# A wider pitch for the split value weights, and one set of five places for the sums of two passes

## The chip, the cores and the metric

The kernel runs on one core of one Trainium2 chip. The metric is the device time of one execution, in microseconds.

## The reference, cut to what matters

One hybrid encoder layer runs over two token sets with shared weights: a long one (1024 tokens, "A" in the kernel) and a short one (512 tokens, "B"). All is float32.

```python
def encoder_layer(x, pre_w, w_in, ...):
    h = rms_norm(x, pre_w)
    cols = jnp.einsum('bsd,dc->bsc', h, w_in)
    m_qk, m_v, m_o, m_z, m_i, m_f, a_qkv, a_z, gate = jnp.split(cols, ..., axis=-1)
    y_m = mlstm_mixer(m_qk, m_v, m_o, m_i, m_f, ...) * silu(m_z)
    y_a = dilated_attention(a_qkv, rel_table) * silu(a_z)
    merged = sig(g[:, :, 0]) * (y_m @ w_pm) + sig(g[:, :, 1]) * (y_a @ w_pa)
    return x + rms_norm(merged @ w_out, post_w)
```

The change concerns one part of `h @ w_in` for the long set: the 2576 columns that are wanted with tokens on the partitions. These are 16 gate columns (i, f), the 1024 value columns of the mLSTM and the 1536 value columns of the attention. The kernel calls them the values.

## The kernel before, in words

**Precision.** A float32 product is made of three matmuls (`mm3`, L212 to L214): each operand is split into a high part, rounded by a copy on ScalarE, and a low part, the rest, by a subtraction on DVE. High times high, high times low and low times high are summed in PSUM.

**Values of the long set, about the first 236 us.** The 1024 x 1024 input of the long set and the weights are taken as 2 x 2 blocks, and a block product by seven products in place of eight (a Strassen-like form; the seven combinations of input blocks are `B11, T2, B21, T3, T1, T4, B22`, high and low parts in `H[0]` and `H[1]`, 512 columns a row). The value columns are computed in four groups of 644 (`value_group`, g = 0 to 3), each of two halves of `VW = 322`. A group needs seven combinations of weights, each `[128, 4 x 322]`: four k slices of 322 columns. Each combination is split into a pair of tiles "vhi" and "vlo" (`split`, ScalarE at L466, DVE at L467); there are two buffers of each, so that one is split while the other is multiplied. In `product` the parts of H are the stationary operand, 128 columns of it, and a k slice of "vhi" or "vlo" is the moving one: 4 token tiles x 4 slices x 3 matmuls = 48 matmuls of 322 columns a product. A token tile's sum fills one of eight PSUM banks ("d").

**The sums.** The products of a group are combined in tiles "u2" (four a group) and "u3" (four a group). ScalarE copies the first product into "u2" (L588 in group 0, L619 later), DVE adds others (L610, L633, L651, L670). At the end of a group `out` writes them: gate columns by a copy (L505), mLSTM values split once more into "vz" or "vzm" (L511, L512) and stored from there, attention values stored straight from the sum by SP (L516). Groups 0 and 2 use four tiles "u2", groups 1 and 3 four tiles "u2b". Group 0 also keeps four sums "held" (L599) for later, in tiles "u2b", and before that "u2b" serves for four small diagonal matrices (`diag`, L383) at the very start.

**Memory of this stage.** Pool "vw" lies on the left, behind the pool of the H tiles. It holds, in this order, "vhi" x2, "vlo" x2, "va", "vb", "vsum" (raw weights and their combinations, 10304 bytes a partition each). The pools "x0" (four rows of tokens, later replaced by "more") follow on the left. On the right lies "us" (small norms, "u2", "u2b"), and beside it "x1", later "co".

**The next stage: pairs.** Behind the values, all other projections of the long set are computed by pairs of units. Its pool "pairs" opens on the left once "vw" has been given back, so on the same bytes. A tile there waits for the users of the earlier tiles on its own bytes and for no others. `pair_weights` allocates, in this order, two "pu2" and one "pu3" of 2048 bytes, two "phlb" of 8192, four "pw_raw" of 4096, two "phla" of 8192 and two "psum_w" of 4096, loads the weights of two units into two "pw_raw" (L691, issued by SP, with high priority), splits the first unit's into "phla" (`pair_split`, ScalarE at L677, DVE at L678), and forms sums of both on POOL (L696, L697, L699) into "psum_w", which are split into the second "phla". `unit_pair` then multiplies: the first product takes the first "phla", the second one the split "psum_w". The weights of the first pair are called for ahead of the last sums of group 3 (L670), which are issued on DVE behind the split of "psum_w":

```python
coming = N.pair_weights(U_AQ, U_AQ + 1, sb)
with tc.issue_after(N.split_end.ins):
    for _ in values[3]:
        pass
for x in late:
    with tc.issue_after(coming[1].ins):
        nc.sync.dma_start(*x)
```

The stores that belong to the last two products of group 3 (list `late`, eight of them, issued at L2084) come behind the load of the pair's second unit.

**Order.** The order of TensorE's instructions is that of the program throughout this part. The order on DVE, ScalarE, POOL and SP is made when the kernel is built, by a list scheduler that plays the program through with estimated times; every engine then works its list in order.

Of the kernel before, what the change touches and what calls it, by code (L numbers as in the profile page):

```python
# [22 lines left out]
F32 = mybir.dt.float32  # L23
F32R = mybir.dt.float32r
AF = mybir.ActivationFunctionType
# [4 lines left out]
P = 128  # L30
D = 1024
KT = D // P
BLK = 512
# [12 lines left out]
VS, NV = 430, 2580  # L46
RING = 1024
VW = 322
U_MQ, U_MK, U_MV, U_MO, U_MZ = 0, 8, 16, 24, 32
U_AQ, U_AK, U_AV = 40, 52, 64  # L50
U_AZ, U_GA, U_GB = 76, 80, 88
# [132 lines left out]
class Net:  # L184
# [264 lines left out]
    def value_weights(self, sb):  # L449
        return [sb.tile([P, 2, 4 * VW], F32, name=x, bufs=1) for x in ("va", "vb", "vsum")]  # L450

    def value_group(self, g, T, H, sb, us, co, ps, late=None, begin=None, u3=None, more=None, turn=None):

# [1 line left out]
        nc = self.nc  # L457
        store = nc.sync.dma_start
        N = 4 * VW
        place = lambda: [sb.tile([P, N], F32R, name=x, bufs=2) for x in ("vhi", "vlo")]  # L460
        def split(x, at=None, parts=1):
            hi, lo = at or place()
            with self.tc.high_priority():
                for i in range(parts):
                    c = slice(i * N // parts, (i + 1) * N // parts)
                    ends = (nc.scalar.activation(hi[:, c], x[:, c], AF.Copy),  # L466
                            (nc.gpsimd if i else nc.vector).tensor_sub(lo[:, c], x[:, c], hi[:, c].bitcast(F32)))  # L467
            self.splits = ends
            return hi.rearrange("p (k c) -> p k c", c=VW), lo.rearrange("p (k c) -> p k c", c=VW)

        def opening(g):
            wa, wb = (sb.tile([P, 2, N], F32, name=x, bufs=1) for x in ("va", "vb"))
# [26 lines left out]
        def out(t, blk, jc, c):  # L499
# [15 lines left out]
            if a0 < hi:  # L515
# [1 line left out]

        vz = lambda: (more.tile([P, 2, VW], F32R, name="vzm", bufs=2) if more and next(turn) < 2 else
                      co.tile([P, 2, VW], F32R, name="vz", bufs=3))
        tile_ = lambda name, bufs: (us if name[:2] == "u2" else co).tile([P, VW], F32, name=name, bufs=bufs)  # L520
        u2 = [tile_(("u2", "u2b")[g % 2], 4) for _ in range(4)]
        add = nc.vector.tensor_add
        if g == 0:
            lead()
# [68 lines left out]
            with self.tc.issue_after(low[0]):  # L593
                sub(T1)
            m2 = product(B21, w12, with_m2(), onto=m1)
            held = []
            for t in range(4):
                held.append(tile_("u2b", 4))
                nc.scalar.activation(held[t], m2[t][:, :VW], AF.Copy)  # L599
            m7 = product(T3, w7, with_m7())  # L600
            with self.tc.issue_after(low[1]):
# [11 lines left out]
            co = co()  # L613
        else:
# [10 lines left out]
            co = co()  # L625
            for t in range(4):
                c = tile_("co", 3)
# [1171 lines left out]
    def place(self, which, i, dt=F32R):  # L1799

        return self.take((("V0b", "V1b", "K0", "K1"), ("H0", "H1", "H2", "H3"))[which][i], dt).rearrange("p (k t) -> p k t", k=4)
# [183 lines left out]
def body(tc, a):  # L1985
# [3 lines left out]
    with ExitStack() as st:  # L1989
# [12 lines left out]
        with ExitStack() as s1:  # L2002
# [4 lines left out]
            with ExitStack() as sv:  # L2007
                vw = N.pool(sv, "vw", 1, "left")
                us = N.pool(s2, "us", 1, "right")
                s3, s4 = ExitStack(), ExitStack()  # L2010
                begin = [vw.tile([P, 4 * VW], F32R, name=x, bufs=2) for x in ("vhi", "vlo")], *N.value_weights(vw)
                r = [us.tile([P, 6], F32, name=f"xr{t}") for t in range(6)]
                one = us.tile([P, VW], F32, name="u2", bufs=4)[0:1, :P]
                diag = [us.tile([P, VW], F32, name="u2b", bufs=4)[:, :P] for _ in range(4)]
                xp = N.pool(s3, "x0", 1, "left"), N.pool(s4, "x1", 1, "right")
                xt = [[xp[i].tile([P, D], F32, name=f"x{i}{t}") for t in range(4)] for i in range(2)]
                minus, plus = (H[1][T4][:, 3, i * P:(i + 1) * P] for i in range(2))
                spare = H[0][T4].bitcast(F32).rearrange("p a c -> p (a c)")
                row, pw = spare[0:1, D:], spare[:, :D]
                rows = lambda i, t: nc.sync.dma_start(xt[i][t], A.x[i * BLK + t * P:i * BLK + (t + 1) * P])  # L2020
                weights = lambda j, kh: nc.sync.dma_start(begin[1 + j][:, kh], a["w_vp"][0, j, kh])
                nc.scalar.dma_start(row, a["prew"][0:1])
                nc.scalar.dma_start(N.prew, a["prewc"])
                for t in range(4):
                    rows(0, t)
                weights(0, 0)
                for t in range(4):
                    rows(1, t)
                for j, kh in ((0, 1), (1, 0), (1, 1)):
                    weights(j, kh)  # L2030
                nc.vector.memset(one, 1.0)
                for i in range(2):
                    p = ps.tile([P, BLK], F32, name="d")
                    nc.tensor.matmul(p, one, row[:, i * BLK:(i + 1) * BLK], start=True, stop=True)
                    nc.vector.tensor_copy(pw[:, i * BLK:(i + 1) * BLK], p)
                nc.scalar.activation(minus, N.ident, AF.Copy, scale=-1.0)
                nc.scalar.activation(plus, N.ident, AF.Copy)
                opened = []

                def co():  # L2040
                    if not opened:
                        s4.close()
                        opened.append(N.pool(s2, "co", 1, "right"))
                    return opened[0]

                def again():
                    H[0][T4] = place("h", T4)

                turns = N.combos(ps, H, xt, r, H[1][T4][:, :2].rearrange("p a c -> p (a c)"), pw, plus, minus, again, diag)
                values = [N.value_group(0, A, H, vw, us, co, ps, None, (*begin, turns), [x[:, :VW] for x in xt[0]])]  # L2050
                next(values[0])
                N.small(N.const)
                N.gate_sums(A, hp)
                N.gate_tile(A, N.const)
                for _ in values[0]:
                    pass
                s3.close()
                more, turn = N.pool(sv, "more", 1, "left"), itertools.cycle(range(5))
                values += [N.value_group(g, A, H, vw, us, co, ps, late if g == 3 else None, more=more, turn=turn)
                           for g in range(1, 4)]  # L2060
                next(values[1])
                with ExitStack() as s4:
                    lanes = N.lanes(A, N.pool(s4, "lane", 1, "right"), lambda: ps.tile([P, BLK], F32, name="d"))
                    for g in range(1, 3):
                        for j, _ in enumerate(values[g]):
                            if j % 3 == 0:
                                with tc.issue_after(N.splits[0].ins), tc.issue_after(N.splits[1].ins):
                                    next(lanes, None)
                    for _ in lanes:
                        pass  # L2070
                    with tc.issue_after(N.splits[0].ins):
                        N.halved()
                    N.bias_tables(N.pool(s4, "tab", 1, "right"), ps, dram)
                for _ in range(7):
                    next(values[3])
# [205 lines left out]
```

## Time and profile before

| | us |
|---|---|
| median of 3 runs | 2209.26 |
| lowest, highest | 2207.99, 2214.44 |
| profiled execution | 2210.35 |
| its span, first to last instruction | 2208.6 |

The page and the answers drawn from the trace are read as follows. A line of a timeline gives the start in us, the duration in us, the engine, the line of the kernel, the operation, the tile written and the tiles read ("out<-in", buffer numbers left out), the shapes, the count, and in brackets the idle time of the engine before it and what ended that. PE is TensorE's matmul, PEld its weight load, ACT ScalarE, DVE VectorE, POOL GpSimd, SP SyncE, "SPq" an engine's DMA-issuing queue. A line of a table by tile or source gives duration min/median/max in ns and the first and last start. Matmuls overlap: a duration is longer than the distance between two starts, and it is the distance that counts. Tiles "u2" of the code stand as "u" in many lines of the trace, since lists of tiles share a name.

### The profile page before, as it was taken

How to read it: one execution, taken by the hardware profiler on the slowest of the kernel's cores; microseconds unless marked ns; L12 is line 12 of the kernel's file. 1: busy time of each engine (PE TensorE's matmuls, PEld its weight loads, DVE VectorE, ACT ScalarE, POOL GpSimd, SP SyncE). 2: the span in 40 equal slices, each digit the busy share in tenths (PEclk: the TensorE clock that was granted, in tenths of full speed). 3: DMA queues.
4: the chain of work that ended last, by engine and by line, in shares of the span. 5: the costliest groups of instructions: out<-in, count | busy, mean ns of one | idle time of the engine just before them, and what ended most of it. 6: DMA issues, size and time to landing. Idle time of an engine off the chain costs nothing.

```text
span 2208.6 us, 34775 instructions
## 1 busy us (share of the span) xinstructions
PE 2188.1 (99%) x12106; PEld 1895.0 (86%) x12106; DVE 1488.0 (67%) x2973; ACT 1102.8 (50%) x2294; POOL 714.5 (32%) x1005
## 2 busy tenths in 40 slices
PE   9999999999999999999999999999999999999998
PEld 8999888888888888888888889998788888888787
DVE  7775675657777656547888765564689845665674
ACT  7332334444444333446676666666666644544332
POOL 1000432333333222326777640011155522232221
PEclk9999999999999999999999999999999999999999
DMA  3742443423323222375745569996868696686663
GB/s 125 194 115 80 158 162 131 172 105 115 115 105 115 86 80 85 132 255 200 242 154 202 160 193 253 249 233 182 256 224 273 198 276 213 214 266 195 233 218 109
DMA packets 209146, 390.45 MB, mean 177 GB/s; under 512 B 37417, under 2 KB 123113, under 8 KB 208970
## 3 DMA queue, kind: packets, MB, share of 16 engines
q1 hardware_dynamic: 179128, 279.63, 40.1%
q0 software_dynamic: 26240, 96.00, 13.8%
q10 hardware_dynamic: 3602, 12.59, 1.4%
q8 instruction: 96, 1.57, 0.3%
q14 instruction: 80, 0.66, 0.1%
HBM read 274.70 MB, written 113.44 MB: 176 GB/s over the span
## 4 chain that ended last, share of the span: by engine, by line
PE 93%; DMA 2%; DVE 2%; ACT 1%; issue 1%; POOL 0%; SPq 0%; DVEq 0%; POOLq 0%; ACTq 0%
PE d L214 14%; PE d L212 14%; PE d L213 14%; PE dense L212 12%; PE dense L213 12%; PE dense L214 12%; PE lg L1486 2%; PE num L214 1%; PE num L212 1%; PE num L213 1%; PE pt L1516 1%; PE a L1095 1%; PE kv L212 1%; PE kv L213 1%; PE kv L214 1%
## 5 line engine op out<-in xcount | busy, mean ns | idle before, releaser
L212 PE MATMUL dense<-H,wh 128*128 128x512 f32 x664 | 270.0, 407 | 0.0
L214 PE MATMUL dense<-H,wl 128*128 128x512 f32 x664 | 260.6, 392 | 0.0
L213 PE MATMUL dense<-H,wh 128*128 128x512 f32 x664 | 260.6, 392 | 0.0
L213 PE MATMUL d<-Hl,phla 128*128 128x512 f32 x608 | 236.5, 389 | 0.0
L214 PE MATMUL d<-Hh,phla 128*128 128x512 f32 x608 | 236.5, 389 | 0.0
L212 PE MATMUL d<-Hh,phla 128*128 128x512 f32 x608 | 236.5, 389 | 0.0
L281 DVE TENSOR_TENSOR wl<-wraw,wh 128x1024 fp32r<-128x1024 f32 (+1 forms) x121 | 148.8, 1231 | 61.2 <-ACT wh L275 61.0
L212 PE MATMUL d<-Hh,phlb 128*128 128x512 f32 x456 | 177.4, 389 | 0.0
L213 PE MATMUL d<-Hl,phlb 128*128 128x512 f32 x456 | 177.4, 389 | 0.0
L214 PE MATMUL d<-Hh,phlb 128*128 128x512 f32 x456 | 177.4, 389 | 0.0
L275 ACT ACTIVATE wh<-wraw 128x1024 fp32r<-128x1024 f32 (+1 forms) x124 | 128.2, 1035 | 69.0 <-PE dense L213 26.3
L214 PEld LDWEIGHTS dense<-H,wl 128*128 128x128 f32 x664 | 124.7, 188 | 27.9
L696 POOL TENSOR_TENSOR psum_w<-pw_raw 128x512 f32<-128x512 f32 x38 | 54.6, 1436 | 282.9 <-DMA pw_raw<-w_in 252.2
L214 PE MATMUL d<-vhi,Hl 128*128 128x322 f32 x448 | 140.5, 314 | 0.5 <-DVE Hl L432 0.3
L212 PE MATMUL d<-vhi,Hh 128*128 128x322 f32 x448 | 140.3, 313 | 0.1
L213 PE MATMUL d<-vlo,Hh 128*128 128x322 f32 x448 | 139.6, 312 | 0.0
L212 PEld LDWEIGHTS dense<-H,wh 128*128 128x128 f32 x664 | 125.1, 188 | 16.0 <-issue 1.2
L213 PEld LDWEIGHTS dense<-H,wh 128*128 128x128 f32 x664 | 125.3, 189 | 14.4
L214 PEld LDWEIGHTS d<-Hh,phla 128*128 128x128 f32 x608 | 114.1, 188 | 23.7
L212 PEld LDWEIGHTS d<-Hh,phla 128*128 128x128 f32 x608 | 114.1, 188 | 23.7
L213 PEld LDWEIGHTS d<-Hl,phla 128*128 128x128 f32 x608 | 114.1, 188 | 23.6
L1505 DVE CUSTOM_DVE_ANT_0 ls<-lg,bias 128x256 f32<-128x256 f32 (+2 forms) x240 | 78.7, 350 | 79.7 <-PE lg L1486 57.9
(605 smaller groups left out, 5945.5 us busy)
## 6 DMA issues: line engine op xcount, KB each, us to landing
pw_raw<-w_in SPq DMA_DIRECT2D x76, 512.0 KB, 4.1
wraw<-w_in SPq DMA_DIRECT2D x63, 512.0 KB, 4.5
aqk_a<-pwk SPq DMA_DIRECT2D x40, 512.0 KB, 3.5
wraw<-w_pm POOLq DMA_DIRECT2D x24, 512.0 KB, 5.7
wraw<-w_out POOLq DMA_DIRECT2D x24, 512.0 KB, 4.0
aqk_b<-sw SPq DMA_DIRECT2D x40, 256.0 KB, 5.9
wraw<-w_v POOLq DMA_DIRECT2D x22, 430.0 KB, 6.3
qk_a<-pwk SPq DMA_DIRECT2D x16, 512.0 KB, 2.6
```

What stands on the lines that cost most here:

```text
L212: nc.tensor.matmul(out, lh, rh, start=start, stop=False, **kw)
L213: nc.tensor.matmul(out, lh, rl, start=False, stop=False, **kw)
L214: nc.tensor.matmul(out, ll, rh, start=False, stop=stop, **kw)
L275: high = nc.scalar.activation(hi[:, :n], raw[:, :n], AF.Copy)
L281: low = (self.lows or nc.vector).tensor_sub(lo[:, :n], raw[:, :n], hi[:, :n].bitcast(F32))
L696: self.nc.gpsimd.tensor_add(s[:, 0], ws[1][:, 0], ws[1][:, 1])
L1095: nc.tensor.matmul(p[:, c - c0], kT[:, ct, c * P:(c + 1) * P], qT[:, ct, c * P:(c + 1) * P], start=ct == 0, stop=ct == 1)
L1486: nc.tensor.matmul(lg[:, hh], q[hh][:, qs], z.rearrange("p (n j) -> p n j", j=P)[:, pair], start=z is k[hh], stop=z is not k[hh])
L1505: nc.vector.tensor_tensor_reduce(out=ls[rows, hh], in0=ts["lg"][hh][rows, of], in1=bt[rows, hh, by], scale=1.0, scalar=NEG, op0=OP.add, op ...
L1516: nc.tensor.transpose(pp[:, hh * nk + x], ts["ls"][:, hh, x * P:(x + 1) * P], self.ident)
```

## The change

The tiles "vhi" and "vlo" get 4 x 384 columns, of which each k slice uses 322; `split` writes 4 runs of 322 and slices k where it sliced columns. The tag "u2b" is gone: all groups take their four sums from one tag "u2" with five places in rotation. The four `diag` matrices come from the same tag. `held` is written into the second halves of the token rows `xt[0]`, beside "u3" of group 0, which is in their first halves as before.

```diff
--- before.py
+++ after.py
@@ -46,6 +46,7 @@
 VS, NV = 430, 2580
 RING = 1024
 VW = 322
+VP = 384
 U_MQ, U_MK, U_MV, U_MO, U_MZ = 0, 8, 16, 24, 32
 U_AQ, U_AK, U_AV = 40, 52, 64
 U_AZ, U_GA, U_GB = 76, 80, 88
@@ -449,7 +450,7 @@
     def value_weights(self, sb):
         return [sb.tile([P, 2, 4 * VW], F32, name=x, bufs=1) for x in ("va", "vb", "vsum")]
 
-    def value_group(self, g, T, H, sb, us, co, ps, late=None, begin=None, u3=None, more=None, turn=None):
+    def value_group(self, g, T, H, sb, us, co, ps, late=None, begin=None, u3=None, held=None, more=None, turn=None):
 
 
 
@@ -457,16 +458,17 @@
         nc = self.nc
         store = nc.sync.dma_start
         N = 4 * VW
-        place = lambda: [sb.tile([P, N], F32R, name=x, bufs=2) for x in ("vhi", "vlo")]
+        place = lambda: [sb.tile([P, 4 * VP], F32R, name=x, bufs=2) for x in ("vhi", "vlo")]
         def split(x, at=None, parts=1):
-            hi, lo = at or place()
+            hi, lo = (z.rearrange("p (k c) -> p k c", c=VP)[:, :, :VW] for z in at or place())
+            x = x.rearrange("p (k c) -> p k c", c=VW)
             with self.tc.high_priority():
                 for i in range(parts):
-                    c = slice(i * N // parts, (i + 1) * N // parts)
-                    ends = (nc.scalar.activation(hi[:, c], x[:, c], AF.Copy),
-                            (nc.gpsimd if i else nc.vector).tensor_sub(lo[:, c], x[:, c], hi[:, c].bitcast(F32)))
+                    k = slice(i * 4 // parts, (i + 1) * 4 // parts)
+                    ends = (nc.scalar.activation(hi[:, k], x[:, k], AF.Copy),
+                            (nc.gpsimd if i else nc.vector).tensor_sub(lo[:, k], x[:, k], hi[:, k].bitcast(F32)))
             self.splits = ends
-            return hi.rearrange("p (k c) -> p k c", c=VW), lo.rearrange("p (k c) -> p k c", c=VW)
+            return hi, lo
 
         def opening(g):
             wa, wb = (sb.tile([P, 2, N], F32, name=x, bufs=1) for x in ("va", "vb"))
@@ -517,8 +519,8 @@
 
         vz = lambda: (more.tile([P, 2, VW], F32R, name="vzm", bufs=2) if more and next(turn) < 2 else
                       co.tile([P, 2, VW], F32R, name="vz", bufs=3))
-        tile_ = lambda name, bufs: (us if name[:2] == "u2" else co).tile([P, VW], F32, name=name, bufs=bufs)
-        u2 = [tile_(("u2", "u2b")[g % 2], 4) for _ in range(4)]
+        tile_ = lambda name, bufs: (us if name == "u2" else co).tile([P, VW], F32, name=name, bufs=bufs)
+        u2 = [tile_("u2", 5) for _ in range(4)]
         add = nc.vector.tensor_add
         if g == 0:
             lead()
@@ -593,9 +595,7 @@
             with self.tc.issue_after(low[0]):
                 sub(T1)
             m2 = product(B21, w12, with_m2(), onto=m1)
-            held = []
             for t in range(4):
-                held.append(tile_("u2b", 4))
                 nc.scalar.activation(held[t], m2[t][:, :VW], AF.Copy)
             m7 = product(T3, w7, with_m7())
             with self.tc.issue_after(low[1]):
@@ -2008,10 +2008,10 @@
                 vw = N.pool(sv, "vw", 1, "left")
                 us = N.pool(s2, "us", 1, "right")
                 s3, s4 = ExitStack(), ExitStack()
-                begin = [vw.tile([P, 4 * VW], F32R, name=x, bufs=2) for x in ("vhi", "vlo")], *N.value_weights(vw)
+                begin = [vw.tile([P, 4 * VP], F32R, name=x, bufs=2) for x in ("vhi", "vlo")], *N.value_weights(vw)
                 r = [us.tile([P, 6], F32, name=f"xr{t}") for t in range(6)]
-                one = us.tile([P, VW], F32, name="u2", bufs=4)[0:1, :P]
-                diag = [us.tile([P, VW], F32, name="u2b", bufs=4)[:, :P] for _ in range(4)]
+                one = us.tile([P, VW], F32, name="u2", bufs=5)[0:1, :P]
+                diag = [us.tile([P, VW], F32, name="u2", bufs=5)[:, :P] for _ in range(4)]
                 xp = N.pool(s3, "x0", 1, "left"), N.pool(s4, "x1", 1, "right")
                 xt = [[xp[i].tile([P, D], F32, name=f"x{i}{t}") for t in range(4)] for i in range(2)]
                 minus, plus = (H[1][T4][:, 3, i * P:(i + 1) * P] for i in range(2))
@@ -2047,7 +2047,8 @@
                     H[0][T4] = place("h", T4)
 
                 turns = N.combos(ps, H, xt, r, H[1][T4][:, :2].rearrange("p a c -> p (a c)"), pw, plus, minus, again, diag)
-                values = [N.value_group(0, A, H, vw, us, co, ps, None, (*begin, turns), [x[:, :VW] for x in xt[0]])]
+                values = [N.value_group(0, A, H, vw, us, co, ps, None, (*begin, turns),
+                                         *([x[:, c:c + VW] for x in xt[0]] for c in (0, BLK)))]
                 next(values[0])
                 N.small(N.const)
                 N.gate_sums(A, hp)
```

## The prediction

> **What bounds the kernel now.** I read the page's first lines and its chain first, then busy time by stage, then the spacing of matmuls in the timeline, then the hand-over from the value stage to the stage behind it.
>
> ```profile
> span 2208.6 us, 34775 instructions
> PE 2188.1 (99%) x12106; PEld 1895.0 (86%) x12106; DVE 1488.0 (67%) x2973; ACT 1102.8 (50%) x2294; POOL 714.5 (32%) x1005
> ...
> PE 93%; DMA 2%; DVE 2%; ACT 1%; issue 1%; POOL 0%; SPq 0%; DVEq 0%; POOLq 0%; ACTq 0%
> ```
>
> TensorE sets the time. A nanosecond off each matmul counts in full, and so does every microsecond in which TensorE waits. The table by stage (window and its length, then busy time and count for PE, PEld, DVE, ACT and POOL, then clock) shows the stage that the change touches:
>
> ```profile
> 13.00:61.10 48.10, 46.68 (x304) 43.39 (x305) 44.64 (x66) 33.22 (x63) 4.61 (x6) 1.00 0.25 79
> 61.10:118.75 57.65, 57.65 (x386) 57.61 (x385) 44.62 (x88) 21.78 (x42) 3.55 (x8) 1.00 0.71 178
> 133.13:235.91 102.78, 102.78 (x681) 101.14 (x680) 60.95 (x103) 25.52 (x34) 9.20 (x9) 1.00 0.35 107
> ```
>
> From 61.1 to 235.9 us TensorE has no gap; before 61.1 it loses 1.4 us. DVE and ScalarE have room. So two things can move the time: the spacing of the 1344 value matmuls (28 products of 48), and a new wait of TensorE.
>
> **The pitch of 384.** With 322 columns the four k slices of a tile begin at 0, 1288, 2576 and 3864 bytes, and the second of the two buffers begins 5152 bytes behind the first; multiples of 64 bytes are hit by the first slice of the first buffer alone. With 384 every slice begins at a multiple of 1536 bytes, and the buffers are 6144 apart. Is there a price for the odd starts? Three consecutive products begin here (start, length of the instruction):
>
> ```profile
> 118.75 0.31 PE L212 MATMUL d<-vhi,Hh 128*128 128x322 f32 x1
> ...
> 125.88 0.31 PE L212 MATMUL d<-vhi,Hh 128*128 128x322 f32 x1
> ...
> 133.13 0.31 PE L212 MATMUL d<-vhi,Hh 128*128 128x322 f32 x1
> ```
>
> The first took 7.13 us, the second 7.25, with the same count and the same clock; they differ in the buffer of the weights. So the place in memory has a price: 148.5 against 151.0 ns a matmul, 149.8 on average. What would an even place cost? In the next stage, where both operands begin at even places, six 512-column matmuls lie between the first pair of rows, and the medians (min/median/max) of three widths follow:
>
> ```profile
> 299.83 0.39 PE L212 MATMUL d<-Hh,phla 128*128 128x512 f32 x1
> ...
> 301.19 0.39 PE L212 MATMUL d<-Hh,phlb 128*128 128x512 f32 x1
> ...
> L214 PE MATMUL d<-Hh,phla x608: 389/389/389, 236.4 to 953.8; 128*128 128x512 f32 x152
> ...
> L214 PE MATMUL d<-vhi,Hl x448: 303/312/417, 13.8 to 235.8; 128*128 128x322 f32 x150
> L214 PE MATMUL num<-ch,ql x160: 277/282/289, 999.1 to 1765.9; 128*128 128x258 f32 x160
> ```
>
> At 512 columns the length never varies, and the spacing is 1.36 / 6 = 226.7 ns. From 258 to 512 columns the length grows by 107 ns, 0.421 ns a column. A regular 322-column matmul would then be spaced 226.7 - 190 x 0.421 = 146.7 ns, 7.04 us a product: 0.09 less than in the better buffer, 0.21 less than in the other, 0.15 on average. Over the 24 products from 61.1 us on that is 3.6 us; the four before it, among transposes and waits, I count at nothing. The bounds: all starts alike could also be alike bad; if every product cost the 7.25 us of the worse buffer, the 28 would lose 28 x 0.06 = 1.7 us. If every matmul were as short as the shortest one (303 against 312), they would gain 1344 x 9 ns = 12.1 us. I take -3.4 us, near the regular row, a little less because 322 is no such round number as 512.
>
> The Trainium skill speaks against any gain here: "TensorE: Matmul & The Clock Gate", section "Step-by-step: what each phase is for", has two independent read ports, so that loading the next weights takes nothing from the running matmul, and its section "Back-to-back issue gap" gives a spacing of N/2.4 + 2.5 ns wherever the operand lies. By that the edit is worth 0 us. The two buffers with 7.13 and 7.25 us don't agree with it.
>
> The splits write 4 runs of 322 instead of one of 1288. They cost 1.28 us on ScalarE and 1.50 on DVE now; an extra of 0 to 0.1 us for three breaks stays beside TensorE, which computes 7 us meanwhile. I take 0.
>
> **The moved tiles: a wait that wasn't there.** The four high and low tiles grow from 5152 to 6144 bytes and take 24576 bytes from the pool's start, not 20608. The pool of the next stage begins at the same byte: two "pu2" and one "pu3" (6144 bytes), two "phlb" (16384), then "pw_raw" from 22528 on. Slots of a tag are handed out first slot first, so the first "pw_raw", which holds the first unit's weights, lies at 22528 to 26624. Before, the low parts ended at 20608. Now the second low buffer is 18432 to 24576 and covers half of that tile; and the last product (m3 of group 3, the 28th) uses second buffers. The load of the first weights must wait until TensorE has read the last low part, where now it is long done:
>
> ```profile
> 223.19 1.78 SPq L691 DMA_DIRECT2D pw_raw<-w_in  x4
> 225.07 4.62 SPq L2084 DMA_DIRECT2D av_a<-u  x4
> ...
> 227.43 1.06 ACT L677 ACTIVATE phla<-pw_raw 128x1024 fp32r<-128x1024 f32 x1 [4.42 <-DMA pw_raw<-w_in]
> ...
> 228.77 1.28 POOL L696 TENSOR_TENSOR psum_w<-pw_raw 128x512 f32<-128x512 f32 x1 [61.77 <-DMA pw_raw<-w_in]
> 230.13 2.15 POOL L697 TENSOR_TENSOR psum_w<-psum_w,pw_raw 128x512 f32<-128x512 f32 x1
> ...
> 229.26 1.87 DVE L678 TENSOR_TENSOR phla<-pw_raw,phla 128x1024 fp32r<-128x1024 f32 x1
> 233.41 1.23 DVE L678 TENSOR_TENSOR phla<-psum_w,phla 128x1024 fp32r<-128x1024 f32 x1 [2.27 <-ACT phla L677]
> 234.55 1.28 DVE L670 TENSOR_TENSOR u2b<-u2b,d 128x322 f32<-128x322 f32 x3
> ...
> 235.61 0.31 PE L213 MATMUL d<-vlo,Hh 128*128 128x322 f32 x1
> 235.76 0.31 PE L214 MATMUL d<-vhi,Hl 128*128 128x322 f32 x1
> 235.91 0.39 PE L212 MATMUL d<-Hh,phla 128*128 128x512 f32 x1
> ...
> DMA to landing us min/median/max: 3.4/4.1/7.4
> ```
>
> (The last row is that of all "pw_raw" loads.) Call T the moment of the first "phla" matmul, 235.91 here. The last low part is read by a matmul that ends at 235.61 + 0.31, so at T. Then: landing 3.4 to 4.1 (the load is alone then, so I lean to 3.7); high part on ScalarE 1.06; two matmuls run on it, but the third needs the low part, on DVE 1.23 to 1.87 (beside POOL's subtraction; 1.7); hand-overs between engines, some 0.5 in all. That third matmul would have begun at T + 2 x 0.227, and begins at T + 7.0: a delay of 6.5 us (5.7 to 7.5).
>
> Queued behind the waiting load on SP: the other three loads, unless they are put ahead of it, and the four late stores, which nobody awaits. Behind the split on DVE: L670's sums of m3, which are issued after the low part of "psum_w". They hold four of eight banks; the fifth product wants the first of these, four products (11 us) on, so it doesn't wait. The second product needs the split "psum_w": POOL 1.3 to 2.15, ScalarE 1.06, DVE 1.23 after the landing, done some 4.5 to 5 us after it; TensorE comes to it 5.5 us or more after the landing. No second wait, if the second unit's load is not held up.
>
> A pause also costs clock. The one stall of this size in the run:
>
> ```profile
> 2098.99 0.63 PE L1746 MATMUL tp<-ident,Q 128*128 128x128 f32 x4 [2.27 <-DVE cw L1720]
> ...
> 2100.42 0.63 PE L213 MATMUL dense<-K,wh 128*128 128x512 f32 x1
> ...
> 2103.41 0.56 PE L214 MATMUL dense<-V0b,wl 128*128 128x512 f32 x1
> 2103.80 0.39 PE L212 MATMUL dense<-V0b,wh 128*128 128x512 f32 x1
> ...
> 2100.00:2105.00 5.00, 5.00 (x17) 3.92 (x16) 4.90 (x11) 2.12 (x2) 0.55 (x2) 0.66 1.04 384
> ```
>
> After 2.27 us without work the matmuls took 0.63 us instead of 0.39 for 3.4 us: eight spacings in 3.38 us, where 0.227 each would make 1.8. One such stretch costs 1.6 us, two 3.2; the pause here is thrice as long, and I take 2.4, between them.
>
> **The sums in five places.** Group g+1 takes one free place and three that group g gives back. At the boundary of groups 0 and 1:
>
> ```profile
> 87.47 0.42 ACT L619 ACTIVATE u2b<-d 128x322 f32<-128x322 f32 x1
> ...
> 91.27 0.42 ACT L619 ACTIVATE u2b<-d 128x322 f32<-128x322 f32 x1
> 92.51 0.46 ACT L511 ACTIVATE vz<-u 128x306 fp32r<-128x306 f32 x1 [0.82 <-DMA vs_a<-vz]
> ...
> 97.04 0.39 PE L212 MATMUL d<-vhi,Hh 128*128 128x322 f32 x1
> ```
>
> The fourth copy (91.27) now waits for the third old sum, whose last reader starts at 92.51: some 2 to 3 us later. Behind it on ScalarE are more such copies; TensorE wants that bank only three quarters through the product that begins at 97.04. Cost 0, and 0 to 1 us if a split is queued behind it. "held" moves onto the second halves of the first x rows, read out by then: 0.
>
> **The sum.** -3.4 + 6.5 + 2.4 = +5.5 us. The profiled execution took 2210.35 us (span 2208.6 and 1.75 around it) and would take 2215.9; the median of the runs shown, 2209.26, is 1.1 lower, so 2214.8. No change, for a measurement of this kernel, is about 0.3%, 6.6 us either way, 2202.6 to 2215.9: the forecast lies just inside its slow edge.
>
> **The rivals.**
> 1. The pace doesn't depend on the start, or all starts are alike and no better; the wait stays: 0 to +1.7, + 8.9: 2218.2 to 2219.9, slower. For it: 512-column matmuls keep 226.7 ns where 512 x 0.421 is 215.6, so even places have a surplus too. Against it: 7.13 against 7.25. It decides once the gain is under 2.3 us. The Trainium skill's spacing rule, cited above, is this case. Chance 0.15.
> 2. A second wait: all four loads stay behind the waiting one, the second unit lands 1.5 us later, and the second product waits 1 to 2 us: 2217, slower. Against it: a slow clock gives it time. Chance 0.10.
> 3. No stall: the first weights land in another slot, or the load is hidden. Only -3.4 is left: 2205.9, not slower. For it: four slots, of which one is touched. Chance 0.15.
> 4. Odd starts are the whole surplus over streaming, and the spacing falls to 322 x 0.421 = 135.6 ns: 1344 x 14.2 ns = 19.1 us less, with the stall 2199.1, faster. Against it: the 226.7 at even places. With rival 3's hand-over a gain of 6.7 us would do too. Chance 0.10.
>
> **How the numbers follow.** The forecast has 0.50. Its terms add up to +2.5 to +9 us, 2211.8 to 2218.3; two fifths of it lie beyond the edge, 0.20, and 0.30 within. Faster: rival 4, 0.10. Same: 0.30 and rival 3, 0.45. Slower: 0.20 and rivals 1 and 2, 0.45. The range runs from rival 3, 2205.5, to between the two ends of rival 1, 2219.5; outside it are rival 4 and the ends of rival 1 and the forecast, together under 0.2.
>
> **What would show it.** Right: products from 61 us on of 7.0 to 7.1 us, equal in both buffers; the first "pw_raw" issued only where the last value matmul ends, then 6 to 7 us with two matmuls, then 0.63 us matmuls for 3 to 7 us; the value stage's end some 3 us earlier. Wrong: two lengths of product as now, "pw_raw" issued ten microseconds ahead of the end of the value stage, or any new wait before 230 us.

## The result, and the profile after

The kernel after took 2216.99 us (median of 22 runs, 2212.38 to 2222.54), the kernel before 2212.01 us in the same series (22 runs, 2207.99 to 2217.51): a ratio of 1.0026, 95% interval 1.0019 to 1.0033, so 4 to 7 us longer. That is less than the 0.3% that the prediction took as the edge, but 22 runs of each tell it from nothing. The prediction's absolute times start from 2209.26 us, the median of three runs; over 22 runs its median is 2.8 us higher, so differences are compared here. The profiled execution after took 2219.36 us. The page's first lines and its chain:

```profile
span 2217.6 us, 34778 instructions
PE 2191.6 (99%) x12106; PEld 1895.8 (85%) x12106; DVE 1487.3 (67%) x2973; ACT 1100.9 (50%) x2294; POOL 714.0 (32%) x1005
...
PE 91%; DMA 5%; DVE 1%; ACT 1%; issue 1%; POOL 0%; SPq 0%; DVEq 0%; POOLq 0%; ACTq 0%
```

TensorE's busy share is the same 99%. In the chain, transfers rise from 2% to 5% of the span. That is some 65 us, far more than the time lost: the chain follows one path back, and where two end at nearly the same time it takes the other by little. It says where to look, for a transfer that TensorE waits for, and not how much it costs.

**The value stage became a little shorter.** The starts of the same three products of the timeline after, in the prediction 7.13 and 7.25 us apart (the lines of `mm3` are one higher in the kernel after, L213 to L215):

```profile
117.68 0.31 PE L213 MATMUL d<-vhi,Hh 128*128 128x322 f32 x1
...
124.80 0.31 PE L213 MATMUL d<-vhi,Hh 128*128 128x322 f32 x1
...
131.92 0.31 PE L213 MATMUL d<-vhi,Hh 128*128 128x322 f32 x1
```

Both buffers now give 7.12 us, 148.3 ns a matmul. T is, as in the prediction, the moment at which the first "phla" matmul would follow without a gap, one spacing of 0.15 us behind the start of the last value matmul. From the first product without a gap to T the stage takes 173.2 us (60.61 to 233.77) instead of 174.8 (61.12 to 235.91): 1.6 us gained. T is 2.1 us earlier; the other half microsecond is the start of that first product, which falls anywhere from 60.2 to 61.7 us in the profiled executions of this study, whatever the edit, and is not read.

**The hand-over became much longer.** What SP's queue waited for between 215 and 237 us, after (us in total, times, longest):

```profile
SPq L691 <- PE d L215: 11.4, 1, 11.4
```

Before, no such line exists. The load of the first pair's weights stood 11.4 us in SP's queue until TensorE had done its last value matmul. The timeline after, around T = 233.77:

```profile
233.62 0.30 PE L215 MATMUL d<-vhi,Hl 128*128 128x322 f32 x1
233.82 1.78 SPq L691 DMA_DIRECT2D pw_raw<-w_in  x4
237.41 1.06 ACT L677 ACTIVATE phla<-pw_raw 128x1024 fp32r<-128x1024 f32 x1 [16.40 <-DMA pw_raw<-w_in]
238.50 1.23 DVE L678 TENSOR_TENSOR phla<-pw_raw,phla 128x1024 fp32r<-128x1024 f32 x1 [11.16 <-ACT phla L677]
238.52 0.62 PE L213 MATMUL d<-Hh,phla 128*128 128x512 f32 x1 [4.59 <-ACT phla L677]
238.75 2.10 POOL L696 TENSOR_TENSOR psum_w<-pw_raw 128x512 f32<-128x512 f32 x1 [73.25 <-DMA pw_raw<-w_in]
238.94 0.63 PE L214 MATMUL d<-Hl,phla 128*128 128x512 f32 x1
239.78 0.80 PE L215 MATMUL d<-Hh,phla 128*128 128x512 f32 x1 [0.21 <-DVE phla L678]
...
240.94 1.28 POOL L697 TENSOR_TENSOR psum_w<-psum_w,pw_raw 128x512 f32<-128x512 f32 x1
...
241.65 0.63 PE L213 MATMUL d<-Hh,phla 128*128 128x512 f32 x1
242.08 0.44 PE L214 MATMUL d<-Hl,phla 128*128 128x512 f32 x1
242.25 1.06 ACT L677 ACTIVATE phla<-psum_w 128x1024 fp32r<-128x1024 f32 x1 [3.78 <-POOL psum_w L697]
...
243.06 0.40 PE L215 MATMUL d<-Hh,phla 128*128 128x512 f32 x1
243.34 1.23 DVE L678 TENSOR_TENSOR phla<-psum_w,phla 128x1024 fp32r<-128x1024 f32 x1 [3.62 <-ACT phla L677]
243.36 0.19 PEld L213 LDWEIGHTS d<-Hh,phla 128*128 128x128 f32 x1 [0.35 <-ACT phla L677]
243.36 0.50 PE L213 MATMUL d<-Hh,phla 128*128 128x512 f32 x1
...
244.62 0.50 PE L215 MATMUL d<-Hh,phla 128*128 128x512 f32 x1 [0.53 <-DVE phla L678]
```

The bracket of each line is the idle time before it and what ended it. Read from the top: the loads leave 0.05 us after T; TensorE stands 4.59 us until the high part of the first weights is made; then it waits for the low part; its matmuls last 0.63 us until 242.08 in place of 0.39, and start 0.43 us apart in place of 0.227, which is half the clock; and at 243.36 and 244.62, in the second product, it waits again, for the parts of "psum_w" (its weight load 0.35 us, then a matmul 0.53 us). Whatever the single waits are called, their sum can be read from one distance: S, from T to the first "phlb" matmul (the third product). The windows of that stretch, before (first line) and after (its length, then busy time of PE, PEld, DVE, ACT and POOL, then clock):

```profile
235.91:244.07 8.16, 8.16 (x39) 6.76 (x37) 3.71 (x3) 2.18 (x3) 4.65 (x4) 1.00 0.65 209
```

```profile
233.77:249.74 15.97, 10.64 (x38) 7.47 (x37) 7.62 (x8) 4.29 (x5) 10.91 (x7) 0.89 0.67 219
```

S went from 8.16 to 15.97 us: 7.8 us lost, 1.6 won before, half a microsecond of chance: the third product begins 5.7 us later in these two executions (249.74 against 244.07). The median says +5.0. The difference stays at 5.7 us for the next 700 us. Behind that the two executions drift against each other at several places, by 0.2 to 2.4 us at a time and in both directions; one profile of each cannot say what of that is chance, and nothing is read from it.

### The profile page after: what moved, and what is told of

It is laid out like the page before. It is cut to its first block, busy times and chain, and to the rows that moved or that the text cites. A ratio compares the mean times of both kernels' runs of the same rounds, so it can differ in the third digit from the quotient of the medians.

```text
span 2217.6 us, 34778 instructions
## 1 busy us (share of the span) xinstructions
PE 2191.6 (99%) x12106; PEld 1895.8 (85%) x12106; DVE 1487.3 (67%) x2973; ACT 1100.9 (50%) x2294; POOL 714.0 (32%) x1005
## 4 chain that ended last, share of the span: by engine, by line
PE 91%; DMA 5%; DVE 1%; ACT 1%; issue 1%; POOL 0%; SPq 0%; DVEq 0%; POOLq 0%; ACTq 0%
PE d L215 14%; PE d L213 14%; PE d L214 14%; PE dense L213 12%; PE dense L214 11%; PE dense L215 11%; PE lg L1486 1%; PE num L215 1%; PE num L213 1%; PE num L214 1%; PE pt L1516 1%; PE a L1095 1%; PE kv L213 1%; PE kv L214 1%; PE kv L215 1%
## 5 line engine op out<-in xcount | busy, mean ns | idle before, releaser
L213 PE MATMUL dense<-H,wh 128*128 128x512 f32 x664 | 270.1, 407 | 0.0
L215 PE MATMUL dense<-H,wl 128*128 128x512 f32 x664 | 260.7, 393 | 0.0
L213 PE MATMUL d<-Hh,phla 128*128 128x512 f32 x608 | 237.3, 390 | 4.6 <-ACT phla L677 4.6
L215 PE MATMUL d<-Hh,phla 128*128 128x512 f32 x608 | 237.3, 390 | 0.7 <-DVE phla L678 0.7
L215 PE MATMUL d<-Hh,phlb 128*128 128x512 f32 x456 | 177.4, 389 | 0.0
L213 PE MATMUL d<-Hh,phlb 128*128 128x512 f32 x456 | 177.4, 389 | 0.0
L215 PEld LDWEIGHTS dense<-H,wl 128*128 128x128 f32 x664 | 124.7, 188 | 28.0
L215 PE MATMUL d<-vhi,Hl 128*128 128x322 f32 x448 | 139.6, 312 | 0.5 <-DVE Hl L433 0.3
L213 PE MATMUL d<-vhi,Hh 128*128 128x322 f32 x448 | 140.0, 312 | 0.1
L213 PEld LDWEIGHTS d<-Hh,phla 128*128 128x128 f32 x608 | 114.4, 188 | 28.8 <-ACT phla L677 5.2
L213 PEld LDWEIGHTS dense<-H,wh 128*128 128x128 f32 x664 | 125.1, 188 | 16.0 <-issue 1.2
L215 PEld LDWEIGHTS d<-Hh,phla 128*128 128x128 f32 x608 | 114.4, 188 | 25.7 <-DVE phla L678 1.9
```

Source lines behind the costliest of these rows:

```text
L213: nc.tensor.matmul(out, lh, rh, start=start, stop=False, **kw)
L215: nc.tensor.matmul(out, ll, rh, start=False, stop=stop, **kw)
```

## The experiments

The theory was the prediction's: the overlap of the first "pw_raw" with the second low buffer makes the stall, the places of the slices make the pace, the sums in five places cost nothing. Each run is judged by S, by the length V of the value stage (first product without a gap to T), by the length of its products, and by the ratio to the kernel before.

| kernel | products, two buffers | V | S | ratio to before, 95% |
|---|---|---|---|---|
| before | 7.13, 7.25 | 174.8 | 8.16 | 1 |
| after | 7.12, 7.12 | 173.2 | 15.97 | 1.0026 [1.0019, 1.0033] |
| e1_room | 7.12, 7.12 | 173.2 | 8.20 | 0.9993 [0.9980, 1.0005] |
| e2_old_pitch_wide | 7.09, 7.11 | 172.8 | 16.02 | 1.0019 [1.0008, 1.0029] |
| e3_sums_only | 7.13, 7.25 | 174.8 | 8.16 | 1.0000 [0.9990, 1.0011] |
| e4_pitch336 | 7.13, 7.14 | 173.5 | 8.21 | 0.9985 [0.9974, 0.9996] |
| e5_busy_pause | 7.12, 7.12 | 173.2 | 16.05 | 1.0033 [1.0021, 1.0045] |
| e6_second_load_early | 7.12, 7.12 | 173.2 | 15.86 | 1.0025 [1.0015, 1.0034] |
| e7_early_and_busy | 7.12, 7.12 | 173.2 | 14.34 | 1.0036 [1.0022, 1.0050] |
| e8_pitch322_room | 7.09, 7.11 | 172.8 | 8.21 | 0.9990 [0.9980, 0.9999] |
| e9_even_base | 7.13, 7.13 | 173.5 | 8.19 | 0.9996 [0.9987, 1.0005] |
| e10_odd_base | 7.13, 7.16 | 173.8 | 8.16 | 0.9999 [0.9987, 1.0011] |
| e11_pitch324 | 7.07, 7.16 | 173.1 | 8.18 | 0.9992 [0.9982, 1.0002] |

**e1_room: only the overlap taken away.** The next stage gets one more "pu3" ahead of its weights, which moves the first "pw_raw" up to 24576 bytes, where the low parts end.

```diff
-        us = [sb.tile([P, BLK], F32, name=f"pu{i}", bufs=4 - i) for i in (2, 3)]
+        us = [sb.tile([P, BLK], F32, name=f"pu{i}", bufs=2) for i in (2, 3)]
```

> The changed kernel with 2048 bytes more in front of the tile pw_raw (two buffers pu3 instead of one), so that no weight load of the pair stage lies on the low parts any more. Theory (the whole loss is the load that waits for the bytes of the last low part): the four loads are issued about 10 us ahead of the end of the value stage again, TensorE passes from the last value matmul to the first phla matmul without a gap, no half clock there, products stay at 7.12 us; time 7 to 8 us below the changed kernel, 2 us below the kernel before: ratio to before 0.9985 to 0.9995. Rival (the wait comes from the order of the lists or from the new rotation of the sums, not from the bytes): the gap of 4.6 us stays, ratio 1.002 to 1.003.

The loads leave early again, 12.6 us ahead of T = 234.78; its timeline has

```profile
222.21 1.79 SPq L691 DMA_DIRECT2D pw_raw<-w_in  x4
```

TensorE has no wait at the hand-over any more, S is 8.20 us, and the whole loss is gone. The stall comes from the shared bytes and from nothing else in the change.

**e2_old_pitch_wide: the tiles stay wide, the pitch goes back to 322.** The kernel after, with

```diff
-            hi, lo = (z.rearrange("p (k c) -> p k c", c=VP)[:, :, :VW] for z in at or place())
+            hi, lo = (z[:, :N].rearrange("p (k c) -> p k c", c=VW) for z in at or place())
```

> The changed kernel with the wide tiles (4 x 384 columns) and the five places, but k slices at a pitch of 322 inside them. Theory (two effects that add, a gain of the pitch of 2 us and a loss of the wait of 7 us; and the second buffer was the slow one because it began at an odd multiple of 32 bytes): the wait and the half clock stay as in the changed kernel, all products cost the 7.13 us of the better buffer before, so the gain is lost by 0.01 us a product only: ratio to before 1.002 to 1.003, like the changed kernel. Rival 1 (the pitch inside the tile is what counts, not where a buffer begins): products of 7.19 us on average, 1.7 us more than the changed kernel, ratio about 1.0035. Rival 2 (the pitch brings the wait): no wait, ratio 0.999.

Three product starts of its timeline:

```profile
118.35 0.31 PE L213 MATMUL d<-vhi,Hh 128*128 128x322 f32 x1
...
125.46 0.31 PE L213 MATMUL d<-vhi,Hh 128*128 128x322 f32 x1
...
132.55 0.31 PE L213 MATMUL d<-vhi,Hh 128*128 128x322 f32 x1
```

7.11 and 7.09 us: not slower than at a pitch of 384 but slightly faster. So the even starts of the slices, for which the change has its pitch, are not what quickened the products; it is that the buffers lie elsewhere. (The 7.09 and the 7.11 don't belong to one buffer each, here and in e8: both values occur in both buffers over the 24 products.) The stall stays: the four loads leave at 234.23, again behind T, which is 234.19 here, and S is 16.02 us. Its slow stretch is longer than that of the kernel after, 5.7 us against 3.6:

```profile
238.97 0.80 PE L213 MATMUL d<-Hh,phla 128*128 128x512 f32 x1 [4.62 <-ACT phla L677]
...
244.66 0.46 PE L213 MATMUL d<-Hh,phla 128*128 128x512 f32 x1
```

S is the same nevertheless, a first sign that something other than the clock sets it.

**e3_sums_only: the kernel before, with the five places for the sums and "held" in the rows of x.** Of its edit, the main lines:

```diff
-        u2 = [tile_(("u2", "u2b")[g % 2], 4) for _ in range(4)]
+        u2 = [tile_("u2", 5) for _ in range(4)]
```

> The kernel before with the five places in rotation and held in the rows of x, and the old pitch and tiles. Theory (this part is free): products of 7.13 and 7.25 us as before, no new gap of TensorE, ratio to before 0.9993 to 1.0007. Rival (the fourth copy of the sums, which now waits for the group before, holds a split back and TensorE waits): a gap of 0.5 to 3 us at a group's start, ratio 1.0003 to 1.0015.

Products, S and V are those of before, the ratio is 1.0000. The rotation costs nothing and brings nothing.

**e4_pitch336: the pitch that fits.** `VP = 336` in place of 384: slices still begin at multiples of 64 bytes, and the low parts end at 21504, below the first "pw_raw".

> The changed kernel with a pitch of 336 columns, 1344 bytes, 21 times 64: k slices begin at multiples of 64 bytes, but not of 512. The low parts end at 21504 bytes of the pool, in front of pw_raw at 22528. Theory (a multiple of 64 bytes is all that the moving operand wants, and without the overlap there is no wait): products of 7.12 us in both buffers, no gap at the hand-over, ratio to before 0.9985 to 0.9995. Rival (multiples of 512 bytes count): products of 7.13 to 7.25 us, ratio 0.9995 to 1.0003.

It is faster than both kernels, by little: 0.9985 [0.9974, 0.9996], and it has no stall. Its products take 7.13 to 7.14 us, between what the theory had (7.12) and the lower end of the rival, so they don't decide between the two.

**e5_busy_pause, e6_second_load_early, e7_early_and_busy: what the stall is made of.** Two causes hang on the first wait: TensorE's half clock after it, and a second wait, since the second unit's load stayed behind the first one's in SP's queue. e5 fills the pause with twenty matmuls whose result nobody reads, to keep the clock up; e6 lets ScalarE's queue issue the second unit's load, which then is done ahead of T; e7 does both.

```diff
+                p = ps.tile([P, BLK], F32, name="d")
+                for i in range(20):
+                    nc.tensor.matmul(p, H[0][B11][:, 0, :P], H[0][B11][:, 1], start=i == 0, stop=i == 19)
```

```diff
-                last = self.nc.sync.dma_start(w, self.a["w_in"][u].rearrange("p (a c) -> p a c", a=2))
+                last = (self.nc.scalar if u == U_AQ + 1 else self.nc.sync).dma_start(w, self.a["w_in"][u].rearrange("p (a c) -> p a c", a=2))
```

> The changed kernel with 20 matmuls more (128 x 512, 4.5 us, their sum is read by nobody) between the last value product and the first pair product, so that TensorE is busy in the pause and its clock need not fall. Measured by S, from the place where the first phla matmul would follow without a gap (233.77 in the changed kernel) to the first phlb matmul, three products on: 8.2 us in the kernel before, 15.97 in the changed one. Theory (behind the pause stands a second wait: the second unit's load was queued behind the first, and its sum is split only 10.8 us after the pause begins; the slow clock runs beside that and costs next to nothing): no 0.63 us matmuls, S 15.6 to 15.9, ratio to before 1.0015 to 1.003. Rival (as the prediction summed it, the slow clock adds to the wait): S 14.2 to 14.5, ratio 1.0008 to 1.0022.

> The changed kernel with the load of the second unit of the first pair issued by ScalarE in place of SP, so that it isn't queued behind the load that waits. Theory (the second wait comes from the queue): the first unit's load still waits for the last low part, but lands a little sooner; the second product has its split before TensorE gets there; the half clock stays. S (15.97 us in the changed kernel) 14.7 to 15.1. Rival (the queue costs nothing, the second wait is POOL's and DVE's time alone): S 15.8 to 16.0.

> Both edits: the 20 matmuls more in the pause, and the second unit's load on ScalarE's queue. Theory: with the second wait gone the clock counts: S 13.5 to 13.9 us, 1.0 to 1.4 less than with the early load alone; what is left over the 8.2 us of the kernel before, 5.5 us, is landing, ScalarE and DVE of the first unit. Rival (the clock doesn't fall for a pause of this size, or rises by itself): the same S as with the early load alone.

The three S are 16.05, 15.86 and 14.34 us. e5 lies a little above its theory (15.6 to 15.9), e6 above its theory (14.7 to 15.1) and in the range of its rival, and e7 above its theory (13.5 to 13.9). The granted clock from 234 to 244 us (the 1.00, 0.83 or 0.70 behind POOL's count) in the kernel after, in e5_busy_pause and in e2_old_pitch_wide, in this order:

```profile
234.00:244.00 10.00, 5.27 (x14) 3.23 (x14) 1.89 (x2) 2.61 (x3) 5.17 (x4) 0.83 0.82 275
234.00:244.00 10.00, 8.10 (x32) 5.40 (x30) 2.25 (x2) 3.17 (x4) 5.62 (x4) 1.00 0.84 276
234.00:244.00 10.00, 5.34 (x14) 3.61 (x13) 1.45 (x2) 2.18 (x3) 4.73 (x4) 0.70 0.82 275
```

With the busy pause the slow matmuls are gone, and S is not a bit shorter. The second wait has grown instead; two lines of the timeline of e5_busy_pause:

```profile
243.00 0.50 PE L213 MATMUL d<-Hh,phla 128*128 128x512 f32 x1 [1.04 <-ACT phla L677]
...
244.26 0.50 PE L215 MATMUL d<-Hh,phla 128*128 128x512 f32 x1 [0.52 <-DVE phla L678]
```

So in the kernel after the second wait sets the time. The third matmul of the second product, the first that reads the low part of "psum_w", starts 10.85 us behind T in the kernel after (244.62), 10.93 in e5 (T = 233.33) and 11.00 in e2 (245.19), with slow stretches of 3.6, 0 and 5.7 us. The clock is hidden behind it.

With the early load that second wait is gone, and S is still 15.86. The timeline of e6_second_load_early, with T = 234.48: the second unit's load, and then the slow stretch:

```profile
220.50 0.33 ACTq L691 DMA_DIRECT2D pw_raw<-w_in  x1
...
238.51 1.06 ACT L677 ACTIVATE phla<-pw_raw 128x1024 fp32r<-128x1024 f32 x1 [16.79 <-DMA pw_raw<-w_in]
239.62 0.79 PE L213 MATMUL d<-Hh,phla 128*128 128x512 f32 x1 [4.98 <-ACT phla L677]
...
240.95 2.18 DVE L678 TENSOR_TENSOR phla<-psum_w,phla 128x1024 fp32r<-128x1024 f32 x1
...
243.70 0.63 PE L215 MATMUL d<-Hh,phla 128*128 128x512 f32 x1
244.12 0.44 PE L213 MATMUL d<-Hh,phla 128*128 128x512 f32 x1
```

The parts of "psum_w" are complete at 243.13, well before the second product, but the clock is half until 244.12. Two things take back what the early load gave. The first load landed 0.4 us later than in the kernel after (the high part begins 4.0 us behind T instead of 3.6), and with it the first product's third matmul started 0.5 us later (240.97, 6.49 behind T, instead of 6.01). And the clock, no longer hidden, shows: from that matmul to the third product e6 takes 9.4 us, the kernel after 10.0. Only with both changes does S fall, by 1.6 us to 14.34; T is 234.55 there, and its third product begins at

```profile
248.88 0.39 PE L213 MATMUL d<-Hh,phlb 128*128 128x512 f32 x1
```

From the third matmul on, that is 7.8 us, against 7.7 in the kernel before. So the slow clock and the second wait ran beside each other: the wait alone costs 2.3 us there (e5), the clock alone 1.7 (e6), both together 2.3 (the kernel after). Each of these is one profiled execution, and the slow stretch is not equally long in each. What is left in e7, 14.34 against 8.16, is the first wait: 6.0 of these 6.2 us lie ahead of the third matmul. Of the 1.6 us the total of e7 shows nothing; its ratio is no lower than that of e6, the intervals overlap, and it rests on four runs. That stays open.

**e8_pitch322_room: the old pitch in tiles of 1408 columns, with the five places.** `VP = 352` and the edit of e2: the tiles end at 22528, just where the first "pw_raw" begins.

> The changed kernel with tiles of 1408 columns (5632 bytes, 11 times 512), k slices at the old pitch of 322, five places in rotation. The low parts end at 22528 bytes, just where pw_raw begins. Theory (the place where a buffer begins is what counted, the pitch in it does nothing): products of 7.09 to 7.11 us in both buffers as with the wide tiles at the old pitch, no wait at the hand-over, ratio to before 0.998 to 0.9995, the best of all. Rival (the pitch of 384 is worth something of its own once the wait is gone): products above 7.12 us.

No stall, products as in e2, 0.9990 [0.9980, 0.9999]. With e4 it is a version that beats both kernels, though its interval ends only just below 1: wider tiles that end below the first "pw_raw" have the gain and not the stall.

**e9_even_base, e10_odd_base, e11_pitch324: which place makes a product slow?** Of the places so far the slow ones, the second buffers of before, begin 32 bytes behind a multiple of 64. The theory for the last runs was that this decides.

```diff
-        place = lambda: [sb.tile([P, N], F32R, name=x, bufs=2) for x in ("vhi", "vlo")]
+        place = lambda: [sb.tile([P, N + 8], F32R, name=x, bufs=2)[:, :N] for x in ("vhi", "vlo")]
```

(and the same for the first pair of tiles); e10 takes the last N columns of each tile, `[:, 8:]`, in place of the first; e11 is the kernel after with `VP = 324`.

> The kernel before with one thing changed: each vhi and vlo tile is 8 columns (32 bytes) longer, none of which is used, so that both buffers of each begin at a multiple of 64 bytes; pitch 322 and the two sets of four sums stay. Theory (the part of a 64-byte stretch in which a slice begins sets its pace: the second buffers of before began 32 bytes into one): products of 7.09 to 7.13 us in both buffers, the hand-over as before (S, from the last value matmul to the first phlb matmul, 8.1 to 8.3 us, the first pw_raw issued some 12 us ahead of the end of the value stage), the value stage ended 1.5 to 2.1 us earlier, ratio 0.999. Rival (it is the pitch, the tile's larger size, or the sums that brought the one pace): 7.13 and 7.25 us in turn as before, ratio 1.000.

> As e9_even_base, but the 322-column slices begin at the eighth column of the longer tiles, so in all four buffers 32 bytes behind a multiple of 64. Theory: 7.25 us in both buffers, the value stage 1.5 to 2.1 us later than before and 3 to 4 us later than in e9_even_base. Rival (the place of the tiles, not that of the slices): 7.09 to 7.13 us as in e9_even_base.

> The kernel after with a pitch of 324 columns: the four slices of every buffer begin 0, 16, 32 and 48 bytes behind a multiple of 64, and the tiles end below the first pw_raw slot, so no stall. Theory, each slice by itself: the first two slices of a product take 1.77 to 1.78 us for their 12 matmuls, the last two 1.81, a product 7.17 to 7.20 us in both buffers. Rival, the begin of the buffer counts for all its slices: 7.09 to 7.13 us, all slices alike.

e9 came out nearly as the theory had it: 7.13 us in both buffers and 1.3 us off V (1.5 to 2.1 were expected), though the ratio, 0.9996 [0.9987, 1.0005], cannot tell that from nothing. e10 refutes it. Product starts of e10_odd_base, whose slices all lie 32 bytes behind a multiple of 64:

```profile
117.53 0.31 PE L212 MATMUL d<-vhi,Hh 128*128 128x322 f32 x1
...
124.69 0.31 PE L212 MATMUL d<-vhi,Hh 128*128 128x322 f32 x1
...
131.82 0.31 PE L212 MATMUL d<-vhi,Hh 128*128 128x322 f32 x1
```

7.16 and 7.13 us, not 7.25, and V is 1.0 us shorter than before, not longer. And the products of e11_pitch324 differ between the buffers, although both begin at multiples of 64:

```profile
118.60 0.31 PE L213 MATMUL d<-vhi,Hh 128*128 128x322 f32 x1
...
125.67 0.30 PE L213 MATMUL d<-vhi,Hh 128*128 128x322 f32 x1
...
132.83 0.31 PE L213 MATMUL d<-vhi,Hh 128*128 128x322 f32 x1
```

7.07 and 7.16 us, the shortest product of all beside one of the longer ones; the theory had 7.17 to 7.20 in both, its rival 7.09 to 7.13. The place of the buffers changes the pace within 7.07 to 7.25 us, and no rule that was tried says which place is which. What in the place counts is open.

## Why the prediction came out as it did

The forecast was +5.5 us, no change that a measurement can tell for sure but near its slow edge; measured +5.0 (4.2 to 7.3). The first wait was right in mechanism and nearly in size. The gain and the term behind the first wait had the right sign for reasons that didn't hold, and the total came out close because their errors met.

1. **The pitch, -3.4.** Measured -1.6 in the stretch for which it was worked out (V). The step that failed is the spacing of a "regular" matmul, 146.7 ns, drawn between 258 and 512 columns: the matmuls came to 148.3 ns (7.12 us / 48), the pace of the better buffer of before, no better. The reason given, odd starts of slices, fell with e2 and e8, where the old pitch in other buffers is the fastest pair of products but for one buffer of e11. That both buffers got the better pace, and not the worse one, is luck. Rival 1 (all starts alike and no better) described the pace better than the forecast did. The Trainium skill ("TensorE: Matmul & The Clock Gate", section "Back-to-back issue gap") gives N/2.4 + 2.5 ns, with no term for the operand's place; at 322 columns that makes an estimate of 136.7 ns. The section gives it as the gap of an isolated matmul and says that in a stream of pairs of weight load and matmul, as here, both set the spacing, a limit that the prediction doesn't name. The runs show 147.3 to 151.0 ns (7.07 to 7.25 us a product), longer than the formula has it, and different by place.
2. **The new wait, +6.5.** The third "phla" matmul began 6.01 us after T instead of 0.455: 5.6 us, just below the range of 5.7 to 7.5. The landing (the high part begins 3.6 us after T) and ScalarE's 1.06 were as forecast. The low part took 1.23 us, not 1.7: POOL's first sum came only with the second unit's landing, and this time it was POOL's instruction that was the longer one (2.10 us against 1.28 before). The hand-overs between engines were hardly there.
3. **The clock, +2.4.** The slow stretch was there, 3.6 us long (238.52 to 242.08), with starts 0.43 us apart where no wait lies between (241.65 to 242.08). But the step that set the second wait to nothing failed, and the clock cost nothing beside it. "No second wait, if the second unit's load is not held up" was the condition, and the load was held up: all four loads stood behind the waiting one, and the second unit landed 1.3 us after the first. The prediction had the parts of "psum_w" made 4.5 to 5 us after the landing, with one of POOL's two steps in the sum. Where the second unit is there already, that is so: 4.6 us in e6 (238.51 to 243.13). In the kernel after both steps come behind the second landing (2.10 and 1.28 us), and it is 7.2 us, from 237.41 to 244.57. The rows of before that the prediction shows have the same 7.2 us (227.43 to 233.41 + 1.23), where they cost nothing, being done ahead of T. So the second product waited: its third matmul began at 244.62, 1.56 us behind the last matmul of the first product (243.06), where three spacings of 0.227 make 0.68, and 0.9 us were lost there; the rest of the wait lies under the slow matmuls before it. From the third matmul on, 2.2 us more were lost until the third product (7.8 in all, less 5.6). That is nearly the 2.4 of the clock term, but e5 has the same loss without the slow clock, so the agreement is luck. Rival 2 was right in its mechanism and wrong in its price: it added the second wait to the clock, and they overlap. That the median after, 2216.99, is the 2217 of rival 2 is chance too; in the same series the kernel before took 2.8 us more than the prediction's base.
4. **Splits, sums in five places, "held": 0.** e3 and the unchanged V confirm it.
5. **The sum.** -1.6 + 7.8, less half a microsecond of chance, is +5.7 in the profiles, where -3.4 + 8.9 was forecast: a gain counted 1.8 us too high met a loss counted 1.1 us too high. That the total is so near is in part luck. Rival 3 failed in the first loads, which left at T, and rival 4 in the pace. Rival 1 came close: the gain stayed below the 2.3 us from which it was to decide, and had the loss been the 8.9 us that it shared with the forecast, the total would have been past the edge.

What would show it was named well for the hand-over (loads at T, two matmuls before the wait, 0.63 us matmuls) and badly for the value stage: 7.0 to 7.1 us a product and three microseconds were asked for, 7.12 and two were seen.

## What to carry to other kernels

Before a tile is made wider, add up where the pool ends and which tile of the next stage will lie on the new bytes; 2048 bytes of overlap cost more here than the change could win, and a pitch of 336 would have done. A load that waited in SP's queue held up the loads behind it, also one that was free to go: issued from ScalarE's queue, the second unit's load left 14 us ahead of T (e6). When a load moves, follow all that hangs on it to the end, also the chain that was early before: here 7.2 us that cost nothing became the wait that set the time. And delays that run side by side are not to be added: the late operand hid TensorE's slow clock here, so take one of them away on paper and ask what the other then costs.

## What the runs showed of the hardware

- The pace of identical matmuls depends on where the moving operand's buffers lie: 7.07 to 7.25 us for 48 matmuls of 322 columns with the same count and clock. The pitch of the slices is not what decides, nor is a begin 32 bytes behind a multiple of 64; the cause is open.
- After a pause of 4.6 us TensorE ran at half its pace for 3.6 us in the kernel after and for 5.7 us in e2_old_pitch_wide, after 5.0 us for 4.5 us in e6_second_load_early. That the stretch varies fits the Trainium skill ("TensorE: Matmul & The Clock Gate", section "Part 1: The HAM clock gate"), by which activity is watched in free-running windows of about 3.4 us, so that the first matmul may fall anywhere in one. Twenty matmuls whose result nobody reads, put into the pause, kept the clock at 1.00 in the window from 234 to 244 us, where the kernel after has 0.83.
